# The output, up and down projections of a hybrid attention block: one planned list in place of an order written by hand

## The chip, the cores and the metric

The kernel runs on 1 core of one Trainium2 chip. Its engines run side by side, each through its own fixed queue of instructions: TensorE (PE in the profile, its weight loads PEld), VectorE (DVE), ScalarE (ACT) and GpSimd (POOL); SyncE (SP) issues the DMAs. An instruction that waits holds up all that is queued behind it on its engine. The metric is the device time in microseconds (us), the median of several runs.

## The reference

One layer on 2048 latent tokens of width 1024 and 256 context tokens, then a last RMS norm. The parts that the change touches come after attention and the delta rule:

```python
def conv_ffn(h, w_up, conv_w, conv_b, w_down):
    u = depthwise_conv(h @ w_up, conv_w) + conv_b
    gate, val = jnp.split(u, 2, axis=-1)
    return (jax.nn.silu(gate) * val) @ w_down
...
    lat_out = jnp.concatenate([o_attn, o_gdn], axis=-1) @ w_out
...
        x = x + g1 * lat_out
        x = x + g2 * conv_ffn(modulate(x, norm2_g[l], sh2, sc2), w_up[l], ffn_conv_w[l],
                              ffn_conv_b[l], w_down[l])
...
    return rms_norm(x, final_norm_g)
```

`o_attn` is normalised, `o_gdn` normalised and gated with SiLU(z). The up projection has 2 x 2816 columns, the convolution runs over three positions, and all values are float32.

## The kernel before

**Numbers.** Each float32 operand of these products is split into a float16 part and a float16 rest (`split`: ScalarE makes the first, GpSimd or VectorE the rest), and three matmuls (part by part, part by rest, rest by part) stand for one. Weights are scaled into the float16 range first, by a norm taken on the way: squares on ScalarE, sums on PE, a power of -0.5 on GpSimd, the scaling on ScalarE.

**Two ways to set an order.** The stages up to attention use `Plan` (lines 193 to 404). The program records operations through stand-ins for the engines (`add`) and tiles (`Lazy`); each gets its dependences, its tile's turn in a ring of buffers, and a modelled duration (`cost`, lines 226 to 258). `order` then walks through modelled time: each engine takes the recorded operation that can start first, and among equals the one recorded earlier ("work"). `issue` writes the instructions out in that order. The model's constants are `fixed` and `rate`: attention sets its own at line 1153, `(150, 55, 200, 170, 25)` and 2.34, and a `patience` for GpSimd and ScalarE; the class has `(65, 65, 0, 50, 42)`, 2.4 and none. By `cost`, VectorE takes `fixed[0] + n / 0.96` ns for n elements a partition and `fixed[1]` more for a scalar operand in memory; a two-input GpSimd operation with float16 result takes `60 + 1.95 n`. The three last stages (lines 1563 to 2345) don't use it. There the order of the calls is the order of the instructions, written by hand: generators are advanced one `yield` at a time between the matmuls, with `idle(n)` to put them back.

**Output projection** (`output`, line 1764). For the four token blocks of 512, in the order 1, 0, 2, 3, `mixed` loads the heads' outputs (line 1811), scales them on VectorE (lines 1831, 1834), transposes them on PE (line 1840) and splits them. `weights` makes the eight weight columns during the first block. Eight products of 24 matmuls (line 1934) give a block; VectorE adds the gated result to x (line 1945), and squares are summed for the second norm. `norm_tail` (line 1591) sums them on PE, takes the power on GpSimd (line 1581), spreads it over the partitions on PE (line 1587), scales the block and writes it to DRAM as `h2c`. `blocks` and `plain` read it back (line 1715) and make the up projection's right-hand operands.

**Up projection** (`up_stage`, line 2028). A block j of 2 x 128 columns is one 2 x 2 block product by a Strassen-like scheme with seven products P1 to P7 of 12 matmuls (line 2035) in place of eight; a step is one j with one half (sb) of the tokens. There are 22 x 2 steps. `parts_of` (line 1679) makes the seven left operands of a block: four sums on GpSimd (lines 1692 to 1702) and seven splits (ScalarE line 1614, GpSimd line 1615). A product accumulates onto one of three banks; what is read from a bank in between (line 2083 after P7, for one) must be read before the next product is added to it (P4, in the step after). PE's order in a step is P1, P6, P4 and P3 of the step before, P5, P2, P7. VectorE and ScalarE gather the results in two rows (`ue`), a single pair for all steps; `after` convolves them (ScalarE line 2103, VectorE line 2106 twice each), applies SiLU, splits the product and stores it as `hidc` (line 2122). `row` and `after` copy two border columns from step to step on GpSimd (lines 2052, 2109).

**Down projection** (lines 2267 to 2344). 96 units, each up to eight blocks of one output column for one token block; `leading` and `rest` scale and split the unit's weights two units ahead (four raw and four split buffers), `down` has the matmuls (line 2297). The last norm of a token block runs during the next. The last column is done in two halves, so that the first half's norm lies under the second half's products.

Of the kernel before, what the change touches and what calls it, by code (L numbers as in the profile page):

```python
# [20 lines left out]
P = 128  # L21
# [97 lines left out]
class Lazy:  # L119
# [30 lines left out]
    def bitcast(self, dtype):  # L150
        return self._next(self.shape, lambda x: x.bitcast(dtype), dtype=dtype)
# [270 lines left out]
def kernel(  # L422
# [1147 lines left out]
    p3a = ExitStack()  # L1570
    x3 = p3a.enter_context(tc.tile_pool(name="x3", bufs=2, side="right", reuse_waits="tile"))
    s3 = p3a.enter_context(tc.tile_pool(name="s3", bufs=2, side="right", reuse_waits="tile"))
    RAWB, WSB, XW = 4, 4, 514
    direct = Direct(nc)

    def rstd_made(e, rs_pool, ps, w, tag):

        n = w // P
        rc = e.tile(rs_pool, [P, 2 * n], F32, "nrc", f"nrc_{tag}", 2)
        e.V.tensor_scalar(out=rc, in0=ps[:, :2 * n], scalar1=1.0 / D, scalar2=EPS, op0=ALU.mult, op1=ALU.add)  # L1580
        e.G.tensor_tensor(out=rc, in0=rc, in1=mhalf.broadcast_to([P, 2 * n]), op=ALU.pow)  # L1581
        return rc

    def rstd_spread(e, ps_pool, ps_tag, ps_bufs, rc, w, tag):
        rs = e.tile(ps_pool, [P, 512], F32, ps_tag, f"nrs_{tag}", ps_bufs)
        for i in range(w // P):
            e.PE.matmul(out=rs[:, i * P:(i + 1) * P], lhsT=rc[:, 2 * i:2 * i + 1].broadcast_to([P, P]), rhs=ident, start=True,
                        stop=True)
        return rs[:, :w]

    def norm_tail(e, xv, tb, acc, pool, h2d, wait=1):

        ps = e.tile(psn, [P, 512], F32, "nps", f"nps_b{tb}", 1)
        for j in range(4):
            e.PE.matmul(out=ps[:, 2 * j:2 * j + 2], lhsT=acc[:, j * P:(j + 1) * P], rhs=ones[:, 0:2], start=True,
                        stop=True)
        dg = rstd_made(e, pool, ps, 512, f"b{tb}")
        for _ in range(wait):
            yield
        rs = rstd_spread(e, psn, "nps", 1, dg, 512, f"b{tb}")  # L1600
        yield
        for k in range(KT):
            e.V.scalar_tensor_tensor(out=xv[:, k, :], in0=xv[:, k, :], scalar=aff2[:, k:k + 1], in1=rs,
                                     op0=ALU.mult, op1=ALU.mult)
            e.S.activation(out=xv[:, k, :], in_=xv[:, k, :], func=AF.Identity, bias=mod2[:, 8 + k:9 + k])
            if k % 2:
                e.SY.dma_start(out=h2d[:, k - 1:k + 1, :], in_=xv[:, k - 1:k + 1, :])
            yield
# [3 lines left out]

    def split(lo_e, dst, src):
        S.copy(out=dst[0], in_=src)  # L1614
        lo_e.tensor_tensor(out=dst[1], in0=src, in1=dst[0], op=ALU.subtract)  # L1615
# [13 lines left out]
    up_w, raw_u = {}, {}  # L1629

    def fetch_up(j, rs=range(2)):
        if j < NJ:
            for r in rs:
                t = w3.tile([P, 2, 4, P], F32, tag="raw", name=f"raw_u{j}_{r}", bufs=RAWB)
                raw_u.setdefault(j, []).append(t)
                SY.dma_start(out=t.rearrange("p a k f -> p (a k) f"), in_=wu[2 * j + r])

    def scales(j, tag):

        g, v = raw_u[j]  # L1640
        ss = w3.tile([P, 2], F32, tag="uss", name=f"uss_{j}", bufs=2)
        sg = w3.tile([P, 8], F32, tag="usg", name=f"usg_{j}", bufs=2)
        fw = w3.tile([P, 8], F32, tag="ufw", name=f"ufw_{j}", bufs=3)
        junk = []
        for r, t in enumerate((g, v)):
            junk.append(s3.tile([P, 2, 4, P], BF16, tag=tag, name=f"junk_{j}_{r}", bufs=2))
            S.activation(out=junk[r], in_=t, func=AF.Square, accum_out=ss[:, r:r + 1])
            yield
        yield from idle(4)
        ps = pt3.tile([P, 512], F32, tag="pt", name=f"uns_{j}")  # L1650
        PE.matmul(out=ps[:, 0:2], lhsT=ones, rhs=ss, start=True, stop=True, skip_group_check=True)
        for r in range(2):
            for k in range(8):
                PE.matmul(out=ps[:, 2 + 2 * r:4 + 2 * r], lhsT=junk[r][:, k // 4, k % 4, :], rhs=ones16, start=k == 0, stop=k == 7,
                          skip_group_check=True)
        V.tensor_reduce(out=sg[:, 0:1], in_=ps[:, 0:2], axis=AX, op=ALU.add)
        V.tensor_scalar(out=sg[:, 0:1], in0=sg[:, 0:1], scalar1=WTOP ** -2, scalar2=1e-30, op0=ALU.mult, op1=ALU.add)
        V.tensor_scalar(out=sg[:, 1:3], in0=ps[:, 2:6].rearrange("p (r c) -> p r c", c=2)[:, :, 0], scalar1=1.0, scalar2=1e-30,  # L1658
                        op0=ALU.mult, op1=ALU.add)
        G.tensor_tensor(out=sg[:, 3:6], in0=sg[:, 0:3], in1=mhalf.broadcast_to([P, 3]), op=ALU.pow)  # L1660
        yield from idle(3)
        for t in (g, v):
            S.activation(out=t, in_=t, func=AF.Copy, scale=sg[:, 3:4])
            yield
        V.tensor_tensor(out=sg[:, 1:3], in0=sg[:, 1:3], in1=sg[:, 4:6], op=ALU.mult)
        V.tensor_tensor(out=sg[:, 1:3], in0=sg[:, 1:3], in1=reach[:, 2 * j:2 * j + 2], op=ALU.mult)
        V.tensor_tensor(out=sg[:, 1:3], in0=sg[:, 1:3], in1=offs[:, 2 * j:2 * j + 2], op=ALU.add)
        V.tensor_tensor(out=bet[:, j:j + 1], in0=sg[:, 1:2], in1=sg[:, 2:3], op=ALU.mult)
        V.reciprocal(out=sg[:, 6:7], in_=bet[:, j:j + 1])
        V.reciprocal(out=sg[:, 7:8], in_=sg[:, 3:4])  # L1670
        V.tensor_scalar(out=fw[:, 0:6], in0=cols[:, C_FC + 6 * j:C_FC + 6 * j + 6], scalar1=sg[:, 7:8], scalar2=hinv,
                        op0=ALU.mult, op1=ALU.mult)
        V.tensor_scalar(out=fw[:, 3:6], in0=fw[:, 3:6], scalar1=sg[:, 6:7], scalar2=DTOP, op0=ALU.mult, op1=ALU.mult)
        V.tensor_scalar(out=fw[:, 6:7], in0=cols[:, C_FB + 2 * j + 1:C_FB + 2 * j + 2], scalar1=sg[:, 6:7], scalar2=DTOP,
                        op0=ALU.mult, op1=ALU.mult)
        up_w[j] = fw
        yield

    def parts_of(j):

        g, v = raw_u.pop(j)
        w = [w3.tile([P, 4, 2, 4, P], F16, tag="ws", name=f"ws_u{j}_{i}", bufs=WSB) for i in range(2)]
        at = {n: w[i // 4][:, i % 4] for i, n in enumerate(TOP)}
        up_w[j] = at, up_w[j]
        a11, a12, a21, a22 = g[:, 0], g[:, 1], v[:, 0], v[:, 1]
        s = w[1][:, 3].rearrange("p f k t -> p (f k t)").bitcast(F32).rearrange("p (k t) -> p k t", k=4)

        def put(n, x):
            split(G, [at[n][:, f] for f in range(2)], x)

        put("A11", a11)
        G.tensor_tensor(out=s, in0=a21, in1=a22, op=ALU.add)
        yield
        put("S1", s)
        G.tensor_tensor(out=s, in0=s, in1=a11, op=ALU.subtract)
        G.tensor_tensor(out=a21, in0=a11, in1=a21, op=ALU.subtract)
        yield
        put("S2", s)
        yield
        put("A12", a12)  # L1700
        yield
        G.tensor_tensor(out=a12, in0=a12, in1=s, op=ALU.subtract)
        put("S3", a21)
        yield
        put("A22", a22)
        yield
        put("S4", a12)
        yield

    def staged(sb, n, tb, k0, raw=False):  # L1710
        if raw:
            t = w3.tile([P, 2, 512], F32, tag="raw", name=f"hst{sb}_{n}_{k0}", bufs=RAWB)
        else:
            t = s3.tile([P, 3, 512], F32, tag="oraw", name=f"hst{sb}_{n}_{k0}", bufs=3)[:, 0:2, :]
        SY.dma_start(out=t, in_=h2c[tb, :, k0:k0 + 2, :])
        return t

    def put(blk, n, kp, x, eng):
        split(eng, [blk[n][:, f, 2 * kp:2 * kp + 2] for f in range(2)], x)

    def plain(sb, blk, which):

        got = []
        for n, kp in which:
            tb, k0 = dict(B11=(0, 0), B21=(0, 4), B22=(1, 4))[n]
            got.append((n, kp, staged(sb, "p" + n, 2 * sb + tb, k0 + 2 * kp)))
            if len(got) == 2:
                yield
                put(blk, *got.pop(0), V)
# [677 lines left out]
```

## Time and profile before

| | us |
|---|---|
| median of 3 runs | 3478.06 (3476.42 to 3480.72) |
| the profiled execution, whole | 3474.39 |
| its span, first to last instruction | 3472.6 |
| output projection's body in it | 1781.2 to 2023.5 |
| up projection | 2023.5 to 2997.1 |
| down projection to the last pass | 2997.1 to 3459.2 |

The mean granted TensorE clock is 0.959 of full speed. In the profile a line like "PE ub L2035 <- DVE xa L2083: 71.0, 18, 4.3" says that TensorE stood still before instructions of line 2035 that write the tile ub, until VectorE had done line 2083, for 71.0 us in 18 times, the longest 4.3. In a timeline row stand start, duration, engine, line, operation, output and input, count, and in brackets the idle time before it and who ended it. Lines of planned stages are all 404, the line that issues them.

### The profile page before, as it was taken

How to read it: one execution, taken by the hardware profiler on the slowest of the kernel's cores; microseconds unless marked ns; L12 is line 12 of the kernel's file. 1: busy time of each engine (PE TensorE's matmuls, PEld its weight loads, DVE VectorE, ACT ScalarE, POOL GpSimd, SP SyncE). 2: the span in 40 equal slices, each digit the busy share in tenths (PEclk: the TensorE clock that was granted, in tenths of full speed). 3: DMA queues.
4: the chain of work that ended last, by engine and by line, in shares of the span. 5: the costliest groups of instructions: out<-in, count | busy, mean ns of one | idle time of the engine just before them, and what ended most of it. 6: DMA issues, size and time to landing. Idle time of an engine off the chain costs nothing.

```text
span 3472.6 us, 63367 instructions
## 1 busy us (share of the span) xinstructions
PE 3159.5 (91%) x25496; PEld 2010.1 (58%) x25496; DVE 2307.9 (66%) x3623; ACT 1731.2 (50%) x2665; POOL 1696.9 (49%) x1572
## 2 busy tenths in 40 slices
PE   6799999979999999999868788999988998999998
PEld 3799878857787777767634333444444443444444
DVE  5665677878777779889745656555555556656554
ACT  5443233457777777777643454454454444322221
POOL 4685455447767777777842344444444444000000
PEclk8999999989999999999989889999999999999999
DMA  6223335641222232322144432121221111654642
GB/s 233 88 67 97 121 112 146 195 127 56 82 92 72 88 99 87 103 82 78 50 151 164 161 139 86 61 69 60 71 69 61 61 62 40 244 185 147 209 142 87
DMA packets 241369, 377.00 MB, mean 109 GB/s; under 512 B 21561, under 2 KB 145049, under 8 KB 238241
## 3 DMA queue, kind: packets, MB, share of 16 engines
q1 hardware_dynamic: 239120, 367.52, 32.1%
q0 software_dynamic: 1952, 5.42, 0.6%
q8 instruction: 200, 3.28, 0.4%
q14 instruction: 97, 0.79, 0.1%
HBM read 262.13 MB, written 111.17 MB: 107 GB/s over the span
## 4 chain that ended last, share of the span: by engine, by line
PE 46%; DVE 17%; issue 12%; POOL 11%; ACT 7%; DMA 5%; SPq 0%; POOLq 0%; DVEq 0%; ACTq 0%
PE pdn L2297 13%; PE sc L404 6%; PE ops L404 5%; DVE cv L2106 5%; POOL ws_u L1615 3%; PE sm L404 3%; PE po L404 2%; PE ub L2035 1%; PE pa L404 1%; ACT cv L2103 1%; DVE mx L404 1%; DMA wm<-in_wm 1%; PE pg L534 1%; PE pg L535 1%; PE pg L533 1%
## 5 line engine op out<-in xcount | busy, mean ns | idle before, releaser
L404 POOL TENSOR_TENSOR lp<-p,hp 128x1024 f16<-128x1024 f32 x288 | 622.3, 2169 | 211.0 <-DVE hp L404 67.8
L2035 PEld LDWEIGHTS <-ws_u 128*128 128x128 f16 x3696 | 369.2, 100 | 556.0 <-issue 141.9
L404 DVE TENSOR_REDUCE mx<-sm 128x1 f32<-128x512 f32 x512 | 336.5, 682 | 64.1 <-PE sm L404 62.4
L404 ACT ACTIVATE p<-sc 128x1024 f32<-128x1024 f32 x288 | 295.3, 1025 | 135.5 <-PE sc L404 125.9
L2297 PEld LDWEIGHTS <-ws_d 128*128 128x128 f16 x2178 | 213.4, 98 | 250.5 <-ACT ws_d L1969 7.1
L2106 DVE SCALAR_TENSOR_TENSOR cv<-xa,ufw,cv 128x1024 f32<-128x1024 f32 (+1 forms) x172 | 242.0, 1417 | 166.9 <-ACT cv L2103 152.3
L2297 PE MATMUL pdn<-hid,ws_d 128*128 128x512 f16 (+1 forms) x1584 | 337.8, 373 | 0.0
L1969 ACT CAST ws_d<-raw_d 128x1024 f16<-128x1024 f32 (+1 forms) x96 | 93.5, 974 | 264.8 <-DVE raw_d L1967 220.5
L404 PE MATMUL sc<-q,kh 128*128 128x512 f16 x576 | 219.0, 380 | 5.1 <-ACT p L404 4.0
L404 PE MATMUL sc<-qx,kx 128*128 128x512 f16 x576 | 219.1, 380 | 0.0
L2035 PE MATMUL ub<-xb,ws_u 128*128 128x512 f16 x528 | 146.9, 437 | 67.3 <-DVE xa L2083 67.3
L404 ACT CAST hp<-p 128x1024 f16<-128x1024 f32 x192 | 201.1, 1048 | 3.5
L404 PE MATMUL ops<-vst,hp 128*128 128x65 f16 (+1 forms) x4608 | 191.6, 193 | 6.4 <-DVE vst L404 3.2
L404 PE MATMUL sm<-kh,q 128*128 128x512 f16 x512 | 175.2, 384 | 13.6 <-DVE mx L404 13.3
L404 PEld LDWEIGHTS <-hp 128*128 128x128 f16 x4608 | 169.9, 97 | 23.2 <-DVE hp L404 2.9
L2035 PE MATMUL ua<-blk_a,ws_u 128*128 128x512 f16 x792 | 181.7, 379 | 0.0
L1934 PE MATMUL po<-ol,ws_o 128*128 128x512 f16 x768 | 180.2, 392 | 0.0
L1615 POOL TENSOR_TENSOR ws_u<-raw_u,ws_u 128x512 f16<-128x512 f32 x110 | 153.1, 1407 | 43.7 <-ACT ws_u L1614 43.7
L1581 POOL TENSOR_TENSOR nrc_f<-nrc_f,mhalf 128x8 f32<-128x8 f32 x3 | 7.6, 2527 | 340.1 <-DVE nrc_f L1580 340.1
L1974 DVE TENSOR_TENSOR ws_d<-raw_d,ws_d 128x1024 f16<-128x1024 f32 (+1 forms) x96 | 108.8, 1134 | 78.1 <-ACT ws_d L1969 78.1
L1660 POOL TENSOR_TENSOR usg<-usg,mhalf 128x3 f32<-128x3 f32 x22 | 36.7, 1668 | 240.0 <-DVE usg L1658 240.0
L533 PE MATMUL pg<-hl,ws_g 128*128 128x512 f32 x384 | 152.9, 398 | 0.0
(695 smaller groups left out, 8000.3 us busy)
## 6 DMA issues: line engine op xcount, KB each, us to landing
raw_d<-in_wd SPq DMA_DIRECT2D x64, 512.0 KB
raw_u<-in_wu SPq DMA_DIRECT2D x44, 512.0 KB
hidc<-cv SPq DMA_DIRECT2D x86, 256.0 KB
tk<-gsc SPq DMA_DIRECT2D x34, 512.0 KB
tT<-gsc SPq DMA_DIRECT2D x66, 256.0 KB
wm<-in_wm SPq DMA_DIRECT2D x64, 256.0 KB
gsc<-kd SPq DMA_DIRECT2D x64, 256.0 KB
hid<-hidc SPq DMA_DIRECT2D x8, 2048.0 KB
```

Source lines behind the costliest of these rows:

```text
L404: fn(**{k: v.get() if isinstance(v, Lazy) else v for k, v in kw.items()})
L533: PE.matmul(out=ps, lhsT=hi_l(k), rhs=hi_r(k), start=st, stop=False)
L534: PE.matmul(out=ps, lhsT=hi_l(k), rhs=lo_r(k), start=False, stop=False)
L535: PE.matmul(out=ps, lhsT=lo_l(k), rhs=hi_r(k), start=False, stop=en)
L1615: lo_e.tensor_tensor(out=dst[1], in0=src, in1=dst[0], op=ALU.subtract)
L1660: G.tensor_tensor(out=sg[:, 3:6], in0=sg[:, 0:3], in1=mhalf.broadcast_to([P, 3]), op=ALU.pow)
L1934: PE.matmul(out=ps, lhsT=w[:, x, k, :], rhs=ols[tb][:, y, k, :], start=k + f == 0, stop=k == KT - 1 and f == 2)
L1969: S.copy(out=made[u][:, 0, :n], in_=raws[u][:, :n])
L1974: V.tensor_tensor(out=made[u][:, 1, :n], in0=raws[u][:, :n], in1=made[u][:, 0, :n], op=ALU.subtract)
L2035: PE.matmul(out=ps, lhsT=w[:, x, k, :], rhs=b[:, y, k, :], start=first and k + f == 0, stop=k == 3 and f == 2, skip_group_check=True)
L2106: V.scalar_tensor_tensor(out=f, in0=t[:, 1 - sb + i:1 - sb + i + W], scalar=s.fw[:, 3 * r + i:3 * r + i + 1], in1=f, op0=ALU.mult, op1=ALU ...
L2297: PE.matmul(out=pss[i][:, :c1 - c0], lhsT=ws[:, x, k, :], rhs=h[:, y, :], start=a + k + f == 0, stop=a + k == NJ - 1 and f == 2)
```

## The change

The three stages become one function, `flow(plan)`, that records all its operations in one plan. One call of `issue` sets the order, with "work" as its rule. One set of pools serves from the first to the last (before, two were closed after the up projection and two opened). `Flow` is `Plan` with a price for memsets, a price for DMAs at 300 GB/s in place of 360, and 30 ns for the small bfloat16 matmuls; `fixed`, `rate` and `patience` stay those of the class. The six matmuls of two k-steps, or the twelve of one product P, form a group that isn't broken up.

```diff
+        def parts_of(j):
...
             put("A11", a11)
-        G.tensor_tensor(out=s, in0=a21, in1=a22, op=ALU.add)
+            V.tensor_tensor(out=s, in0=a21, in1=a22, op=ALU.add)
...
-        G.tensor_tensor(out=s, in0=s, in1=a11, op=ALU.subtract)
-        G.tensor_tensor(out=a21, in0=a11, in1=a21, op=ALU.subtract)
+            V.tensor_tensor(out=s, in0=s, in1=a11, op=ALU.subtract)
+            V.tensor_tensor(out=a21, in0=a11, in1=a21, op=ALU.subtract)
...
-        G.tensor_tensor(out=a12, in0=a12, in1=s, op=ALU.subtract)
+            V.tensor_tensor(out=a12, in0=a12, in1=s, op=ALU.subtract)
...
         def row(s, r):
             t = ue[r]
-            if s.sb:
-                G.tensor_copy(out=t[:, 0:2], in_=carry[:, 2 * s.j + r, :])
-            else:
-                G.memset(t[:, 0:2], 0.0)
-            G.memset(t[:, 1026:1028], 0.0)
+            S.copy(out=t[:, 0:2], in_=carry[:, 2 * s.j + r, :] if s.sb else zero)
             return t
...
-                    G.tensor_copy(out=carry[:, 2 * j + r, :], in_=t[:, 1024:1026])
+                    S.copy(out=carry[:, 2 * j + r, :], in_=t[:, 1024:1026])
...
-                G.tensor_copy(out=tailc[:, j, :], in_=z[:, :, 0])
+                V.tensor_copy(out=tailc[:, j, :], in_=z[:, :, 0])
...
+        first, w0, w1 = mixes(order[0]), weights(0), weights(1)
+        for g, n in ((first, 8), (w0, 3), (first, 4), (w1, 3), (first, 4)):
+            for _ in range(n):
+                next(g)
+        plan.gate = len(plan.ops) - 1
...
-                tracks.append(blocks(0, blk0, 1, True))
-                tracks.append(chained(idle(4), scales(0, "osq"), idle(2), parts_of(0)))
-                tracks.append(chained(idle(16), scales(1, "osq")))
+                tracks.append(chained(*(plain(0, blk0, m, kp) for m, kp in (("B11", 0), ("B11", 1), ("B21", 0), ("B21", 1))),
+                                      blocks(0, blk0, 1, V, False), *(plain(0, blk0, "B22", kp) for kp in range(2))))
+                tracks.append(chained(scales(0), parts_of(0), scales(1), parts_of(1)))
...
-            pace = 2
+            pace = 1
             if n == 1:
-                drain(work)
-                fetch_up(2)
-                work = chained(idle(2), scales(2, "nacc"), wd_squares(0), wd_squares(1))
-            elif n == 3:
-                drain(work)
-                work = chained(idle(6), parts_of(2))
+                work = chained(scales(2), parts_of(2), wd_squares(0), wd_squares(1))
             elif n >= 4 and sb == 0 and j < NJ - 3:
                 drain(work)
-                if n == 4:
-                    fetch_up(3)
...
+                work = chained(scales(j + 1), parts_of(j + 1), *(wd_squares(q) for q in more))
...
-                finish(x2, tb, cuts[0], rs, range(0, 4))
+                finish(x2, tb, cuts[0], rs, range(0, KT))
                 down(1, *tails[2])
                 gated(1)
-                squares(1)
-                ps = sums(pt3, "pt", acc[:, 256:512], 256, "fin1")
-                finish(x2, tb, cuts[0], rs, range(4, KT))
...
+        plan.issue(dict(o=("work", 1.0)))
+
+    class Flow(Plan):
+
+        @staticmethod
+        def cost(eng, name, kw, rate, fixed):
+            if name == "memset":
+                return 100.0, 0.0
+            if name.startswith("dma_start"):
+                t = kw["out"]
+                return 60.0, int(np.prod(list(t.shape))) * (2 if t.dtype == F16 else 4) / 300.0
+            if eng == "PE" and name == "matmul" and kw["rhs"].dtype == BF16:
+                return 30.0, 0.0
+            return Plan.cost(eng, name, kw, rate, fixed)
+
+    flow(Flow(tc, psn, pt3, ps3))
```

Matmuls, splits and convolution stay as they were in number and shape. New work is six more reads of `h2c` (512 KB each): the first half's B11, B21 and B22 are staged by themselves (`plain`) in place of being made from tiles that `blocks` holds. Their rests are made on VectorE; before, GpSimd made four of the six. `bitcast` of a recorded tile now gives the shape that the new type has.

More of the change, by code (lines that the diff above doesn't have):

```diff
@@ L1591, in norm_tail @@
[L1591 to L1608, printed above, removed]
@@ L1627, in chained @@
             yield from x
[L1629 to L1647, printed above, removed]
-            yield
[L1649 to L1663, printed above, removed]
-            yield
[L1665 to L1677, printed above, removed]
@@ L1881, in output @@
-        w0, w1 = weights(0), weights(1)
-        first = together([mixed(1, i) for i in range(4)], 2)
-        for n, _ in enumerate(first):
-            if n == 1:
-                for _ in range(2):
-                    load_wo()
-            if n >= 2:
-                next(w0, None)
-            if n >= 4:
-                next(w1, None)
-        drain(w0)
-        drain(w1)
-        new_x(order[0])
-        blk0, blk1 = {}, {}
-        tracks, pend = [], None
+                yield from mixed(tb, i, ols[tb])
@@ L2028, in up_stage @@
-    def up_stage():
-        acc, xv, blk0, blk1, rest0, work = output()
-        def product(ps, w, b, first):
-            for k in range(4):
-                for f, (x, y) in enumerate(((0, 0), (0, 1), (1, 0))):
-                    PE.matmul(out=ps, lhsT=w[:, x, k, :], rhs=b[:, y, k, :], start=first and k + f == 0,
-                              stop=k == 3 and f == 2, skip_group_check=True)
+                blk0.update(four(mk(ol3, [P, 2, 2, 4, 512], F16, "ol", "blk0_a", 4), ("B11", "T2")))
@@ L2038, in up_stage @@
+            if not end:
+                drain(chained(*tracks))
+        rest = tracks
         class Step:
@@ L2271, with last_norm @@
+        def last_norm(x2, tb, acc):
+            yield
+            rc = sums(acc, 512, f"f{tb}")
+            yield
+            yield
+            rs = spread(rc, 512, f"f{tb}")
+            yield
+            finish(x2, tb, (0, 512), rs, range(0, 4))
+            yield
+            finish(x2, tb, (0, 512), rs, range(4, KT))
+            yield
+        pend, x2 = iter(()), None
         for u, (tb, b, a, n) in enumerate(units):
@@ L2300, in gated @@
-            def gated(i, b=b, x2=x2, pss=pss, cuts=cuts, xp=xp):
+                for k0 in range(0, n, 2):
+                    with plan.group():
+                        for k in (k0, k0 + 1):
+                            h = hids[tb][a + k]
+                            for f, (x, y) in enumerate(PAIRS):
+                                PE.matmul(out=pss[i][:, :c1 - c0], lhsT=ws[:, x, k, :], rhs=h[y][:, c0:c1],
+                                          start=a + k + f == 0, stop=a + k == NJ - 1 and f == 2, skip_group_check=True)
```

764 lines of the change are left out of this document (358 added, 406 removed).

## The prediction

> **What bounds the kernel now.** I read the page's engine row first, then the windows view, cut where the kind of TensorE work changes. Its columns: stretch, length, busy us (and instructions) of PE, PEld, DVE, ACT, POOL, granted clock, DMA share, GB/s.
>
> ```profile
> PE 3159.5 (91%) x25496; PEld 2010.1 (58%) x25496; DVE 2307.9 (66%) x3623; ACT 1731.2 (50%) x2665; POOL 1696.9 (49%) x1572
> ...
> 1781.20:2023.50 242.30, 198.77 (x962) 98.04 (x961) 141.45 (x203) 101.64 (x177) 80.60 (x76) 0.92 0.46 164
> 2023.50:2150.00 126.50, 96.56 (x419) 43.47 (x418) 76.80 (x91) 57.14 (x77) 54.84 (x54) 0.85 0.31 106
> 2150.00:2997.10 847.10, 769.28 (x3700) 347.21 (x3699) 495.32 (x683) 392.47 (x526) 362.77 (x449) 0.95 0.21 74
> 2997.10:3025.40 28.30, 21.66 (x90) 8.97 (x89) 15.43 (x14) 8.30 (x9) 0.19 (x1) 0.88 0.61 210
> 3025.40:3459.20 433.80, 433.59 (x2103) 206.52 (x2101) 248.47 (x273) 104.81 (x120) 8.59 (x4) 1.00 0.48 155
> ```
>
> The rows are: the body of the output projection, the first up steps, the other up steps, the hand-over to down, and down. In down PE is busy 433.59 of 433.80 us: nothing is to be had. In the others no engine is full, PE pauses, and the granted clock is under 1: the mark of an order that blocks, not of a full engine. PE's busy time hides part of it, because a matmul at a low clock is busy for longer. So I count the matmuls of the main lines (1934 in the body, 2035 in up) and price them at the full rate.
>
> ```profile
> 1781.20:2023.50 242.30, 179.94 (x768) 0.92 0.46 164
> ...
> 2023.50:2150.00 126.50, 92.90 (x384) 0.85 0.31 106
> 2150.00:2997.10 847.10, 752.25 (x3313) 0.95 0.21 74
> ...
> 2231.56 2.75 PE L2035 MATMUL uc<-blk_b,ws_u 128*128 128x512 f16 x12
> 2234.15 2.75 PE L2035 MATMUL ua<-blk_b,ws_u 128*128 128x512 f16 x12
> ```
>
> Twelve matmuls, one product, start 2234.15 - 2231.56 = 2.59 us after the last: 0.2158 us each. PE's other work in a stretch is its busy time less that of the main line. Lost time of each:
> - Body: 768 x 0.2158 = 165.7, other 198.77 - 179.94 = 18.8, together 184.5 of 242.3: **57.8 lost**.
> - First up steps: 384 x 0.2158 = 82.9, other 3.7, together 86.6 of 126.5: **39.9 lost**.
> - Other up steps: 3313 x 0.2158 = 714.9, other 17.0, together 731.9 of 847.1: **115.2 lost**.
> - Hand-over: 90 x 0.2158 = 19.4 of 28.3: **8.9 lost**.
>
> Together 221.8 us. The waits view says whom PE waited for (us in total, times, longest), and the timeline shows one case from end to end.
>
> ```profile
> PE ub L2035 <- DVE xa L2083: 71.0, 18, 4.3
> PE pto L1840 <- DVE oraw L1831: 18.9, 7, 5.8
> PE nrs_b L1587 <- POOL nrc_b L1581: 12.9, 1, 12.9
> PE ub L2035 <- ACT blk_b L1614: 12.4, 1, 12.4
> PE nps_b L1595 <- DVE nacc_b L509: 10.3, 1, 10.3
> ...
> 2223.35 5.25 PE L2035 MATMUL ub<-xb,ws_u 128*128 128x512 f16 x12 [3.94 <-DVE xa L2083]
> 2251.09 0.68 DVE L2092 TENSOR_TENSOR xa<-uc,u 128x512 f32<-128x512 f32 x1
> 2255.48 1.26 POOL L1702 TENSOR_TENSOR raw_u<-raw_u,ws_u 128x512 f32<-128x512 f32 x1
> 2256.78 0.62 ACT L1614 CAST ws_u<-raw_u 128x512 f16<-128x512 f32 x1 [2.43 <-POOL raw_u L1702]
> 2257.30 1.24 ACT L2103 ACTIVATE cv<-xa,cols,ufw 128x1024 f32<-128x1024 f32 x1
> 2258.58 6.18 DVE L2106 SCALAR_TENSOR_TENSOR cv<-xa,ufw,cv 128x1024 f32<-128x1024 f32 x4 [6.81 <-ACT cv L2103]
> 2266.00 0.69 DVE L2083 TENSOR_TENSOR xa<-ub,s 128x512 f32<-128x512 f32 x1
> 2266.74 4.04 PE L2035 MATMUL ub<-xb,ws_u 128*128 128x512 f16 x12 [3.94 <-DVE xa L2083]
> ```
>
> Read it upwards. PE stands 3.94 us because product P4 may not write its bank before VectorE has read it (line 2083). VectorE is late because four convolution steps came just before, after a wait of 6.81 us for ScalarE. ScalarE had the rows of the convolution at 2251.09 + 0.68 = 2251.77 and took them at 2257.30: its queue held a weight cast that waited for a GpSimd sum (line 1702). So weights for the next block, due much later, hold up this step. This comes once in 43.39 us (2223.35 to 2266.74), one pair of steps.
>
> **Part by part.**
>
> *Other up steps.* The change takes out this chain twice over. Four sums (lines 1692 to 1702) go from GpSimd to VectorE, and the planner puts each operation where its modelled inputs are ready. Is there room? In this stretch there are 20 blocks. VectorE gets the four sums and a two-column tail copy per block, priced at 0.69 each by the 512-wide row above (which reads PSUM; the sums read SBUF): 69 us, so 564; ScalarE gets six two-column copies per block, not in the trace; between 0.19 and 0.62 us each (the cheapest and the narrowest rows below and above) they make 23 to 74 us, so 415 to 467; GpSimd falls. Against 731.9 us of PE work that is 77% and 57 to 64%: PE is what binds, and the copies lie under it, at up to 0.62 us each where that cover fails.
>
> The copies also bring ScalarE a wait that GpSimd had, for the convolution to have read the row (last row of the next fence: 28.2 us in 32 times, 0.9 each). Behind it in ScalarE's queue stand the row's own eviction, which waits for the same reads, and the next block's casts; 40 x 0.9 = 36 us fit into its free 36%. SyncE's queue: with four raw buffers the next block's loads go out about a block (43 us) before use, against landings of 6 to 7 us (below), so a hidden store ahead of them costs nothing; zero.
>
> ```profile
> 2226.15 0.19 ACT L1647 ACTIVATION_READ_ACCUMULATOR junk<-raw_u 128x1 f32 x1
> ...
> 1400.00:1500.00 100.00, 94.05 (x1372) 70.45 (x1370) 86.37 (x145) 69.98 (x92) 76.13 (x40) 1.00 0.29 91
> 1500.00:1600.00 100.00, 96.32 (x1429) 72.02 (x1426) 84.33 (x144) 74.00 (x97) 74.29 (x39) 0.98 0.28 88
> 1600.00:1700.00 100.00, 97.77 (x1446) 74.42 (x1445) 85.19 (x137) 75.34 (x94) 78.99 (x40) 1.00 0.17 54
> ...
> L1615 POOL TENSOR_TENSOR ws_u<-raw_u,ws_u 128x512 f16<-128x512 f32 x82 | 110.2, 1361 | 1.5 <-ACT ws_u L1614 1.5
> L2106 DVE SCALAR_TENSOR_TENSOR cv<-xa,ufw,cv 128x1024 f32<-128x1024 f32 x64 | 98.0, 1551 | 110.3 <-ACT cv L2103 107.1
> ...
> POOL xa L2055 <- DVE cv L2106: 28.2, 32, 1.3
> ```
>
> How well does a planned list do? The attention stage, planned by the same code, keeps PE busy for 94.05, 96.32 and 97.77 of 100 us, with VectorE at 85%, fuller than here. But its model has constants of its own; the new list uses the class's defaults, and by these a GpSimd split costs 60 + 512 x 1.95 = 1058 ns, a convolution step 65 + 1024 / 0.96 + 65 = 1197. The trace has 1361 and 1551. A list made with short durations has operations in the queue before their inputs are there. So I take 95%, under the mean: 731.9 / 0.95 = 770.4, 38.5 lost, **76.7 gained**. Bounds: 97.77% (16.7 lost) and 94.05% (46.3).
>
> What do the pauses left over cost?
>
> ```profile
> 2068.31 0.59 PE L1651 MATMUL uns<-uss,k 128*128 128x2 f32 x2 [2.81 <-ACT junk L1647]
> 2069.19 5.28 PE L2035 MATMUL ua<-blk_b,ws_u 128*128 128x512 f16 x12
> 2074.26 3.04 PE L2035 MATMUL ub<-blk_T,ws_u 128*128 128x512 f16 x12
> ```
>
> A pause of 2.81 us made the next product last 2074.26 - 2069.19 = 5.07 us in place of 2.59: it cost 2.81 + 2.48 = 5.29. [...]
>
> *Body.* Its pauses are of order too: a transpose issued ahead of its VectorE scaling (18.9 us), the norm's spread behind GpSimd's power (12.9), both able to stand behind ready products. What stays is the start, where each weight column must be loaded, squared and scaled. I leave 25 lost: **32.8 gained**. Bounds: 96% busy (184.5 / 0.96, 8 lost) and 45 lost. The new list stages six more tiles of 512 KB; 3.1 MB at the body's 164 GB/s is 19 us of DMA, beside a DMA share of 0.46: hidden, and up to 19 if it is not, since these tiles feed the first up step.
>
> *First up steps.* The path is the last norm, its write to DRAM, the reads back, then the blocks for the second half. The reads:
>
> ```profile
> 1938.99 6.23 DMA hst_b<-h2c
> 2056.62 7.16 DMA hst_b<-h2c
> ```
>
> PE has two steps, 14 x 2.59 = 36 us, to fill that path, and in a planned list four more products that need no difference block (10 us). Today's path also holds pauses that the order makes (10.3, and part of 12.4). I leave 20 lost: **19.9 gained**; bounds 8 and all 39.9. [...]
>
> *Hand-over, down, tail.* Down's prices, buffers (four raw, four split) and order stay: zero, under VectorE's 248 of 433.8 us. Hand-over 8.9 to 6, **2.9 gained** (bounds 3 and 8.9). At the end, eight scalings of the first half now stand together ahead of the last gate:
>
> ```profile
> 3457.07 1.66 DVE L2237 SCALAR_TENSOR_TENSOR x<-x,cols,nrs_fin 128x256 f32<-128x256 f32 x4 [2.86 <-PE nrs_fin L1587]
> 3459.03 0.48 DVE L2302 SCALAR_TENSOR_TENSOR x<-pdn,mod,x1p 128x256 f32<-128x256 f32 x1 [0.31 <-PE pdn L2297]
> ```
>
> Eight take 3.3 us and end at 3460.4, so the gate comes **1.4 later** (bounds 0 and 1.7).
>
> *Sum:* 76.7 + 32.8 + 19.9 + 2.9 - 1.4 = 130.9 us. The profiled execution took 3474.39 us (span 3472.6), the median of the runs is 3478.06, 3.67 more. Profiled after: 3343.5; median: 3347.2. With the good bounds together (98.5 + 49.8 + 31.9 + 5.9 - 1.4 = 184.7) 3293; with the bad ones (68.9 + 12.8 + 0 + 0 - 1.7 = 80.0) 3398.
>
> **Rivals.**
> - *Half the up pauses stay.* The short durations make ScalarE or VectorE stand ahead of the convolution in about every second pair, and body and first steps gain nothing: 115.2 / 2 - 1.4 = 56 gained, 3422. For: 1361 against 1058. Against: VectorE 23% free. Chance 0.12.
> [...]
> - *No change.* The one pair of convolution rows stays single; if its release (convolution read, then the next eviction) were the real cycle, another wait would take the old one's place: 3478. Against: ScalarE's lag of 5.5 us explains the pause alone. Chance 0.03.
> - *Slower.* Sums and splits of weights stand ahead of line 2083 in VectorE's fixed queue in every step, not once per pair. A pause with its slow product costs 3.94 + 2.48 = 6.4 us; 40 of them are 257 lost in place of 115.2, 142 more, and with the other gains, 32.8 + 19.9 + 2.9 - 1.4 = 54.2: about 3566. It decides when the loss per pair exceeds (115.2 + 54.2) / 20 = 8.5 us. Against: VectorE has its one pause per pair now, and the list staggers such work. Chance 0.09.
>
> **Numbers.** The forecast has 0.66. Faster by over 0.2% (7 us, about what a measurement here can tell from none): 0.66 + 0.12 + 0.10 = 0.88; within 0.2%: 0.03; slower: 0.09. The range goes from 3296, the forecast's good end, to 3422, the first rival.
>
> **What would show it.** Right: waits of PE for line 2083's successor under 20 us, clock 0.98 or more in up, PE's pauses for transposes gone, the up steps 770 us long. Down stays at 434. Wrong: a PE wait of some 4 us in every step; VectorE over 85% in up; a long wait of PE for the second half's blocks; a DMA share over 0.7 in the body.

## The result, and the profile after

| | median us (lowest to highest) | ratio to before, 95% interval |
|---|---|---|
| before, on the same chip | 3479.39 (3476.42 to 3484.18) | |
| the planned list | 3281.97 (3278.77 to 3283.9) | 0.943 [0.9414, 0.9447] |

The forecast was 3347, in a range from 3296 to 3422. The time fell by 197, not by 131. The profiled execution took 3278.77 us, its span is 3276.8, and the mean granted clock rose from 0.959 to 0.979. The engine row and the windows of the planned kernel, cut at the same borders as before (ahead of the body stands the ramp, from attention's last matmul):

```profile
PE 3106.2 (95%) x25496; PEld 1995.0 (61%) x25496; DVE 2395.4 (73%) x3737; ACT 1747.1 (53%) x2797; POOL 1550.0 (47%) x1241
...
1745.90:1771.50 25.60, 10.22 (x46) 7.66 (x47) 17.07 (x31) 15.65 (x38) 18.32 (x22) 0.54 0.73 257
1771.50:1958.40 186.90, 185.96 (x959) 94.63 (x960) 144.54 (x217) 100.94 (x172) 78.44 (x73) 0.99 0.64 232
1958.40:2065.00 106.60, 91.81 (x438) 42.34 (x436) 79.90 (x104) 58.04 (x86) 29.67 (x19) 0.94 0.39 132
2065.00:2803.10 738.10, 732.72 (x3653) 337.09 (x3651) 576.04 (x769) 405.36 (x639) 242.75 (x152) 1.00 0.26 86
2803.10:2825.00 21.90, 21.90 (x103) 9.97 (x102) 19.73 (x21) 9.92 (x10) 0.00 (x0) 1.00 0.70 222
2825.00:3262.80 437.80, 437.58 (x2122) 208.30 (x2119) 246.50 (x266) 102.03 (x119) 6.55 (x4) 1.00 0.48 150
3262.80:3276.80 14.00, 1.80 (x8) 1.45 (x8) 5.28 (x14) 0.42 (x1) 1.01 (x1) 0.65 0.44 150
```

In the body and in the other up steps PE is now busy for over 99% of the stretch, at a clock of 0.99 and 1.00. Stage by stage:

| | before | after | change | forecast |
|---|---|---|---|---|
| up to attention's last matmul | 1753.4 | 1745.9 | -7.5 | 0 |
| ramp | 27.8 | 25.6 | -2.2 | 0 |
| output's body | 242.3 | 186.9 | -55.4 | -32.8 |
| first up steps | 126.5 | 106.6 | -19.9 | -19.9 |
| other up steps | 847.1 | 738.1 | -109.0 | -76.7 |
| hand-over | 28.3 | 21.9 | -6.4 | -2.9 |
| down | 433.8 | 437.8 | +4.0 | 0 |
| tail | 13.4 | 14.0 | +0.6 | +1.4 |

Most of the first row is the change too, though the operations of those stages are the same. From the delta rule's last matmul (1700.5 us before, 1698.8 after) to attention's last one, the kernel before takes 52.9 us and so does e1, the other order by hand below; the planned kernels take 46.1 to 49.4, this one 47.3. There the output projection's first loads and scalings stand among attention's last operations, and the list puts them in other places. So some 5.6 of the 7.5 us are a gain that the forecast had at 0; what an execution has won or lost up to 1700 us is spread.

In the row of the other up steps 6.5 us only moved: 43 matmuls of the down projection lay in that stretch before and 13 do now, 30 x 0.2158 us, and hand-over and down have them instead. The excess over the forecast stands in the body, 22.6 us, and in the other up steps, 32.3, or 25.8 without what moved.

Whom PE waits for from 1740 us to the end (total, times, longest):

```profile
PE pto L406 <- DVE oraw L406: 14.4, 7, 5.8
PE nps_b L406 <- DVE nacc_b L406: 5.1, 1, 5.1
PE uns L406 <- ACT junk L406: 4.1, 1, 4.1
PE ub L406 <- ACT blk_b L406: 3.8, 1, 3.8
PE ops L406 <- POOL lp L406: 3.0, 3, 1.2
PE ub L406 <- DVE xa L406: 2.8, 3, 1.5
```

All planned stages have the one line 406, so one goes by the tiles (ub, uc and ua are the up projection's banks). The wait that stood on top, PE for the read of P4's bank, is down from 71.0 us in 18 times to 2.8 in 3. Of the transposes' 14.4 us, 13.6 lie in the ramp; in the body there is one wait of 0.8. One step of the planned list, rows of VectorE and PE from its timeline:

```profile
2402.89 2.17 DVE L406 TENSOR_TENSOR cv<-cv,cv 128x1025 f32<-128x1025 f32 x1
...
2404.99 0.68 DVE L406 TENSOR_TENSOR xa<-ub,s 128x512 f32<-128x512 f32 x1
...
2405.59 1.04 DVE L406 TENSOR_TENSOR raw_u<-raw_u,raw_u 128x512 f32<-128x512 f32 x1
2405.72 2.75 PE L406 MATMUL ub<-blk_T,ws_u 128*128 128x512 f16 x12 [0.19 <-DVE xa L406]
```

The eviction after P7 (xa from ub) ends at 2405.67, and P4 starts at 2405.72: just in time, with nothing in hand. The weight sum (raw_u) stands behind the eviction. In the other step of the pair the eviction ends over 3 us early.

### The profile page after: what moved, and what is told of

The parts are those of the page before. It is cut to its first block, busy times and chain, and to the rows that moved or that the text cites. A ratio compares the mean times of both kernels' runs of the same rounds, so it can differ in the third digit from the quotient of the medians.

```text
span 3276.8 us, 63242 instructions
## 1 busy us (share of the span) xinstructions
PE 3106.2 (95%) x25496; PEld 1995.0 (61%) x25496; DVE 2395.4 (73%) x3737; ACT 1747.1 (53%) x2797; POOL 1550.0 (47%) x1241
## 3 DMA queue, kind: packets, MB, share of 16 engines
q1 hardware_dynamic: 239984, 370.67, 34.8%
## 4 chain that ended last, share of the span: by engine, by line
PE 72%; DVE 12%; POOL 5%; DMA 4%; ACT 3%; issue 3%; SPq 0%; POOLq 0%; DVEq 0%; ACTq 0%
PE pdn L406 14%; PE ub L406 9%; PE sc L406 6%; PE uc L406 6%; PE ua L406 6%; PE po L406 6%; PE ops L406 5%; PE sm L406 3%; PE pa L406 1%; DVE cv L406 1%; DVE mx L406 1%; PE pg L531 1%; PE pg L530 1%; PE pg L532 1%; ACT p L406 1%
## 5 line engine op out<-in xcount | busy, mean ns | idle before, releaser
L406 PEld LDWEIGHTS <-ws_u 128*128 128x128 f16 x3696 | 361.7, 99 | 444.2 <-issue 23.9
L406 DVE SCALAR_TENSOR_TENSOR cv<-xa,ufw,cv 128x1025 f32<-128x1025 f32 (+1 forms) x176 | 251.8, 1486 | 61.2 <-ACT cv L406 61.2
L406 POOL TENSOR_TENSOR ws_u<-raw_u,ws_u 128x512 f16<-128x512 f32 x110 | 181.2, 1655 | 197.4 <-ACT ws_u L406 156.0
L406 PE MATMUL po<-ol,ws_o 128*128 128x512 f16 x768 | 173.4, 382 | 0.0
L406 POOL TENSOR_TENSOR usg<-usg,mhalf 128x3 f32<-128x3 f32 x22 | 20.0, 909 | 285.4 <-DVE usg L406 285.4
L530 PE MATMUL pg<-hl,ws_g 128*128 128x512 f32 x384 | 152.8, 398 | 0.0
L532 PE MATMUL pg<-hl,ws_g 128*128 128x512 f32 x384 | 152.3, 397 | 0.0
```

Source lines behind the costliest of these rows:

```text
L406: fn(**{k: v.get() if isinstance(v, Lazy) else v for k, v in kw.items()})
L530: PE.matmul(out=ps, lhsT=hi_l(k), rhs=hi_r(k), start=st, stop=False)
L532: PE.matmul(out=ps, lhsT=lo_l(k), rhs=hi_r(k), start=False, stop=en)
```

## The experiments

The theory after the result: PE stood still through the order alone, and the planned list gains because it puts weight work behind the eviction that frees PE's bank. Its rivals: the gain comes from the sums' move to VectorE alone; from PE's matmuls being rearranged; or from free room on engines. Four runs took the change apart, six changed the model's durations, and the rest asked how much room VectorE has, and what an order costs. Stage lengths below are taken as in the table above, from the main line's first and last matmuls; the first up steps are its first 384. The last column counts waits for the evictions (tiles xa and u).

| run | median us | body | first up | other up | PE ub <- DVE: us, times |
|---|---|---|---|---|---|
| before | 3478.06 | 242.3 | 126.5 | 847.1 | 71.0, 18 |
| planned list | 3281.97 | 186.9 | 106.6 | 738.1 | 2.8, 3 |
| e1, hand order, sums on VectorE | 3408.96 | 242.4 | 123.3 | 780.9 | 34.8, 20 |
| e2, list, sums on GpSimd | 3305.13 | 187.1 | 109.6 | 753.7 | 11.8, 19 |
| e10, list, PE in recorded order | 3300.26 | 197.2 | 107.7 | 740.1 | 4.2, 3 |
| e7, list by "path" | 3491.95 | 212.6 | 118.4 | 863.4 | 87.7, 36 |
| e4, attention's durations | 3275.17 | 185.2 | 105.4 | 733.6 | 5.1, 3 |
| e8, e4 and dearer two-input work | 3280.72 | 185.5 | 108.5 | 739.1 | 5.5, 2 |
| e6, durations x 1.5 | 3300.64 | 186.4 | 106.9 | 771.2 | 14.1, 4 |
| e13, x 0.9 | 3291.33 | 191.1 | 105.7 | 740.0 | 3.8, 3 |
| e12, x 0.75 | 3398.66 | 199.0 | 112.3 | 833.6 | 70.5, 22 |
| e5, x 0.5 | 3446.69 | 209.0 | 110.9 | 871.1 | 117.5, 22 |
| e11_1, 2 more additions a step, planned | 3282.0 | 186.8 | 105.1 | 737.0 | 4.7, 4 |
| e11_2, 4 more, planned | 3300.85 | 187.2 | 109.0 | 755.9 | 5.4, 5 |
| e14, 4 more, not planned | 3382.34 | 187.0 | 106.3 | 833.8 | 77.1, 25 |
| e9, e4 and patience | 3274.28 | 185.6 | 101.8 | 733.7 | 3.0, 2 |
| e15, planned list again | 3282.95 | 186.6 | 105.4 | 738.6 | 2.8, 3 |
| e16, e9 again | 3272.97 | 185.7 | 101.8 | 733.7 | 3.0, 2 |

**The sums by hand (e1).** Kernel before, with one part of the change: four lines of `parts_of`.

```diff
-        G.tensor_tensor(out=s, in0=a21, in1=a22, op=ALU.add)
+        V.tensor_tensor(out=s, in0=a21, in1=a22, op=ALU.add)
```

and so for the other three sums.

> The order written by hand, with one edit: the four sums of the weights' parts go from GpSimd to VectorE. Theory Q (the GpSimd sums are the cause: ScalarE's casts wait for them and the convolution waits behind the casts): the pause of some 4 us per pair of steps goes, PE's wait for line 2083 falls from 71 us to under 20, and the time to about 3380. Theory O (the order of the queues is the cause, whichever engine has the sums): the casts stay ahead of the convolution in ScalarE's queue and now wait for VectorE; at least half of the 71 us stays, 3425 to 3480.

Measured: 3408.96 us, ratio 0.9795 [0.9778, 0.9812]. The other up steps became 66 us shorter, the body not at all. PE's waits in this kernel, the second row from its body alone (18.9 before):

```profile
PE ub L2035 <- DVE xa L2083: 34.8, 20, 6.6
PE pto L1840 <- DVE oraw L1831: 18.1, 6, 5.8
```

The result lies between what the two theories gave. The same pause still comes once a pair, at 1.25 us for 3.94, and in one case followed through (at 2251.72 us) ScalarE takes the convolution's rows 0.1 us after they are there, where it came 5.5 us late. So ScalarE's wait for the GpSimd sum was the greater part of the up steps' loss, as the prediction's chain of rows said, and that part can be had without a list.

**The list without the sums' move (e2), and PE not rearranged (e10).** e2 is the planned kernel with those four lines back on `G`. In e10 the other engines are planned as in the change, but PE takes only the oldest operation that it has left:

```diff
+                if e == "PE" and self.fifo:
+                    cand = [i for i in cand if i == self.fifo[-1]]
```

> The planned list, with the four sums back on GpSimd. Theory Q: the pauses come back in part, some 2 us a pair, 3310 to 3340. Theory O: the list puts the casts where the sums are done, PE waits no more than in the planned kernel, 3282 within 6.

> The planned list, but PE must take its operations in the order in which they are recorded; the other engines are planned freely. If PE's look-ahead is what removes the pauses (theory L): 3300 to 3350, pauses in every pair. If the order of the other queues is (O): the up steps after the first stay within 5 us of the planned kernel's 738, and only the body and the first up steps lose, some 10 to 25 us together: about 3295.

Measured: 3305.13 (0.9495 [0.9478, 0.9512]) and 3300.26 (0.9484 [0.9465, 0.9503]). e2 again lies between its theories, e10 near its second. With the sums left on GpSimd the list still takes 93 us out of the other up steps; with both it is 109 (6.5 of each only moved). Either part alone breaks most of the chain, so their gains (66 and 93) don't add up to 109. The order alone isn't all, then: which engine makes the sums is worth 66 us by hand and 16 in the list. Rearranging PE is worth 10 us of the body's 55 and 2 us of the other up steps (5, since 12 more of down's matmuls lie in the planned kernel's). In e10 the 308 up products even stand in exactly the order that they had by hand, and the other up steps take 740.1 us in place of 847.1: what gains there is the order of the other engines. For the body e10 shows less. Its recorded order of PE isn't the hand-written one, since the transposes stand elsewhere between the products, so how the other 45 us are shared between that order and the other engines' queues stays open.

**The rule (e7).** One word: the ready operation with the longest modelled path behind it goes first, in place of the one recorded first.

```diff
-        plan.issue(dict(o=("work", 1.0)))
+        plan.issue(dict(o=("path", 1.0)))
```

> The planned list with the rule path (what has the longest chain behind it goes first) in place of work (what is recorded earlier). What is left to win in the planned kernel is some 20 us in the first up steps, which hang on a chain, and 10 elsewhere. If the rule matters: first up steps under 100, total 3265 to 3278. If PE's time is all that counts: 3282 within 5; it may be slower by up to 20 if products of later steps are held back.

Measured: 3491.95 us, ratio 1.0034 [1.0021, 1.0047], a little slower than the order by hand and far outside all that was expected. PE waits in it:

```profile
PE ub L406 <- DVE u L406: 69.7, 27, 4.0
PE pto L406 <- DVE oraw L406: 24.8, 3, 13.7
PE ub L406 <- DVE xa L406: 18.0, 9, 5.7
```

So a planned list as such gains nothing: this one has the same operations, pools and sums on VectorE and the same copies on ScalarE, and is 210 us longer than the change.

**The durations (e4, e8, e6, e5, e12, e13).** The prediction feared that short modelled durations leave 38.5 us of pauses. These kernels have the same operations, and in their model other constants. e4 and e8 start from

```diff
-    flow(Flow(tc, psn, pt3, ps3))
+    listed = Flow(tc, psn, pt3, ps3)
+    listed.fixed = (150, 55, 200, 170, 25)
+    flow(listed)
```

and e8 also makes two-input work dearer, by 1.4 on GpSimd and 1.15 on VectorE. In the planned kernel's other up steps a convolution step on VectorE took 1491 ns on average, 1.17 of e4's 1272: 1283 where GpSimd was busy for under a tenth of it (100 steps), 2144 where for over nine tenths (19). The others have, with 0.5 (e5), 0.75 (e12), 0.9 (e13) or 1.5 (e6),

```diff
-            return Plan.cost(eng, name, kw, rate, fixed)
+            d, move = Plan.cost(eng, name, kw, rate, fixed)
+            return (d if eng in ("PE", "SY") else 0.5 * d), move
```

> The planned list, made with the fixed costs that attention's list uses (150, 55, 200, 170, 25), nearer to the durations in the trace. If short modelled durations cost something (theory S, the 5% of the prediction): faster than the planned kernel by 5 us or more, under 3277. If a list bound by PE has slack for them (theory P): 3282 within 4.

> The planned list, made with attention's fixed costs, and GpSimd's two-input operations at 1.4 and VectorE's at 1.15 of their modelled time, as the trace shows them when both run at once. If what is left of the pauses in the up steps comes from durations that are short (theory S, small): up steps 730 to 733, total 3270. Theory P: no further gain over the list with attention's constants, 3275 within 4.

> The planned list, made with the same durations raised by half, so that by the model VectorE is over-full in the up steps. Theory S: the list is late everywhere, the planner lets PE's products slip back; up steps 760 or more, total over 3310. Theory P: the order stays workable, total 3280 to 3300.

> The planned list, made with VectorE's, ScalarE's and GpSimd's durations halved. Theory S (short durations cost what the prediction gave them): a list that is short by half, not by a tenth, loses far more: up steps 780 to 850 us, total over 3330. Theory P (a stage with slack on the other engines takes almost any list): up steps within 15 us of 738, total under 3305.

> The planned list, made with VectorE's, ScalarE's and GpSimd's durations at three quarters: short by a quarter more than in the planned kernel. With the halved list at 871 us in the up steps and the planned one at 738, a loss that grows evenly with the error (theory S) gives about 800, total about 3350; a loss that starts only where the slack of the other engines is used up (theory P) gives under 755, total under 3305.

> The planned list with the model's VectorE, ScalarE and GpSimd durations times 0.9. With the class's durations the other up steps took 738 us, with three quarters of them 834. Even-loss theory (each per cent by which the durations are too short costs PE something): 738 + 0.4 x 96 = 776 us, the whole about 3320. Step theory (nothing is lost until the list has put weight work ahead of the eviction that frees P4's bank): either 745 or less and the whole under 3290, or at once over 800 and the whole over 3345; nothing between.

Measured, as ratios: e4 0.9409 [0.9392, 0.9426], e8 0.9424 [0.941, 0.9438], e6 0.9481 [0.9466, 0.9497], e5 0.9899 [0.9884, 0.9914], e12 0.9763 [0.9747, 0.978], e13 0.9441 [0.942, 0.9461]. Better durations (e4) are worth some 4 us in the up steps and 7 in the whole. Dearer ones on top (e8) give nothing more: its 739.1 us hold 43 of down's matmuls where the change has 13, and 30 x 0.2158 = 6.5. Ten per cent shorter costs 2 us there and 4 in the body (e13's whole is 1.3 us over the bound set for the step, its up steps are within theirs). A quarter shorter costs 96 and a half 133, both more than either theory had; with the half, the up steps are longer than by hand. So the loss isn't even: 2 us for the first tenth, 94 more between 0.9 and 0.75. What happens there, in the timeline of e12:

```profile
2431.50 2.75 PE L406 MATMUL ub<-blk_b,ws_u 128*128 128x512 f16 x12
2432.73 1.64 DVE L406 TENSOR_TENSOR ws_u<-ws_u,raw_u 128x512 f32<-128x512 f32 x1
2434.29 1.22 DVE L406 TENSOR_TENSOR cv<-cv,cv 128x1025 f32<-128x1025 f32 x1
2435.43 1.64 DVE L406 TENSOR_TENSOR raw_u<-raw_u,ws_u 128x512 f32<-128x512 f32 x1
2436.99 0.68 DVE L406 TENSOR_TENSOR xa<-ub,s 128x512 f32<-128x512 f32 x1
```

Two weight sums of 1.64 us, due later, have passed ahead of the eviction, and P4 starts at 2437.72, after a pause of 3.47 us. That is the mechanism of the prediction's rival "slower", sums ahead of line 2083's successor, though it comes once per pair (22 waits) and not in every step. In e5, where the convolution's last step and the tail copy stand ahead of the eviction as well, this wait reaches 117.5 us, again in 22 times:

```profile
PE ub L406 <- DVE xa L406: 117.5, 22, 9.5
```

Too long durations aren't free either: in e6 the up steps take 771.2 us, with 73 of down's matmuls among them, 60 x 0.2158 = 13 us, so some 20 us go. One wait of 11.3 us for VectorE is in it; which order caused the rest I didn't trace.

**Room or place (e11, e14).** Additions whose results nobody uses are added to VectorE's work: two (e11_1) or four (e11_2) of 511 columns per step, recorded in the plan. The lines of e11_2, which stand in a loop over the two rows of the step (e11_1 has `range(1)`):

```diff
+                if (j, sb) != (0, 0):
+                    for _ in range(2):
+                        V.tensor_tensor(out=c[:, 1025:1536], in0=f[:, 0:511], in1=f[:, 511:1022], op=ALU.add)
```

e14 has the same four per step from block 2 on, but issued right ahead of the eviction after P7, unknown to the plan (the part that issues them):

```diff
+                        if i in self.late:
+                            x = args["out"]
+                            for _ in range(4):
+                                nc.vector.tensor_tensor(out=x[:, 0:511], in0=args["in1"][:, 0:511], in1=args["in1"][:, 1:512], op=ALU.add)
```

> The planned kernel with two more 511-wide additions on VectorE in each up step, results not used; the planner knows of them. VectorE's share of the up steps after the first goes from 78% to about 85%. Theory V (what a planned list loses is set by how full the fullest of the other engines is, and the prediction read its loss from attention's stretches at 85%): up steps 745 to 760. Theory P, taken strictly (PE's time alone counts as long as no engine is full): 738 within 4.

> The same with four more additions per step; VectorE to about 92%. Theory V: PE at 90 to 95%, up steps 770 to 810, total 3315 to 3355. Theory P, taken strictly: still under 750, total under 3295.

> The planned list, and in the steps of blocks 2 to 21 four additions of 511 columns on VectorE (some 0.65 us each, their result is not used) issued right ahead of the eviction after P7, without the plan knowing of them. e11_more_vector_2 has the same four per step, but planned. Amount theory (only VectorE's load counts): other up steps 756 us and the whole 3301, as there. Place theory (in one step of each pair the eviction comes just in time, so what stands ahead of it delays P4): 20 pauses of 2.6 us, other up steps about 790 (780 to 840 if the late evictions also cost clock), the whole 3330 to 3385, and a PE wait for that eviction of 40 us or more in some 20 times.

Measured: 3282.0 (0.9423 [0.9409, 0.9437]), 3300.85 (0.948 [0.9466, 0.9494]) and 3382.34 (0.9701 [0.9679, 0.9724]). The windows from 2100 to 2750 us of e11_1, e11_2 and e14, in this order:

```profile
2100.00:2750.00 650.00, 645.59 (x3243) 298.15 (x3242) 541.38 (x756) 367.38 (x579) 218.48 (x144) 1.00 0.24 74
```

```profile
2100.00:2750.00 650.00, 633.24 (x3178) 290.08 (x3177) 564.35 (x818) 360.62 (x572) 221.49 (x139) 1.00 0.23 71
```

```profile
2100.00:2750.00 650.00, 590.50 (x2894) 268.32 (x2893) 540.58 (x733) 329.84 (x520) 199.81 (x125) 0.97 0.21 65
```

At 541 / 650 = 83% VectorE cost PE nothing (e11_1); at 87% the other up steps were 18 us longer (e11_2), between what the two theories gave. e14 has the additions of e11_2, with VectorE at 83% of its longer steps, and loses 96. So the amount alone doesn't decide; the place does. Its wait and one case of it, VectorE's timeline:

```profile
PE ub L2236 <- DVE xa L2236: 77.1, 25, 4.1
```

```profile
2328.78 2.18 DVE L2236 TENSOR_TENSOR cv<-cv,cv 128x1025 f32<-128x1025 f32 x1
2330.88 3.83 DVE L2235 TENSOR_TENSOR xa<-s 128x511 f32<-128x511 f32 x4
2334.80 0.69 DVE L2236 TENSOR_TENSOR xa<-ub,s 128x512 f32<-128x512 f32 x1
```

The additions took 3.83 us, not the 2.6 expected, and PE's pause is 3.85: once per pair, where the eviction had nothing in hand.

**A better version (e9, e16), beside the change (e15).** e4 with attention's `patience` for GpSimd and ScalarE:

```diff
+    listed.fixed = (150, 55, 200, 170, 25)
+    listed.patience = PATIENCE
```

> The planned list with attention's fixed costs and its patience as well: GpSimd may wait 150 ns and ScalarE 100 for an operation that is more urgent. Both theories: 3275 within 4; faster by 5 or more would say that the greedy choice costs something here.

> The planned list as it was changed, once more, beside e16. 3282 within 4 us.

> The planned list with attention's durations and patience, as in e9_patience. If its gain of 8 us there is real: 3274 within 3 us and an interval wholly under that of e15; if it was chance: the intervals overlap.

Measured: e9 3274.28 (0.9406 [0.9391, 0.942]); on one chip e15 3282.95 (3282.07 to 3283.47, 0.9416 [0.9396, 0.9437]) and e16 3272.97 (3271.18 to 3274.8, 0.9387 [0.9366, 0.9407]). The two ratios' intervals overlap, from 0.9396 to 0.9407, so by the sign set beforehand it isn't decided; both carry the spread of the kernel before. The runs themselves lie 7 us apart. By them e16 is faster by about 0.3%, of which the first up steps give 3.6 us and the other up steps 4.9. What the patience adds to e4 isn't shown: in the whole, e9 and e4 overlap (3272.57 to 3275.03 and 3271.05 to 3277.58). e16 has the lowest median found.

## Why the prediction was right in sign and too small

- **"The mark of an order that blocks, not of a full engine."** Right. In the other up steps the prediction's 731.9 us of PE work are 725.4 without the 6.5 that moved, so PE loses 738.1 - 725.4 = 12.7 us in place of 115.2 (its row shows 5.4 idle), and in the body 186.9 - 184.5 = 2.4 in place of 57.8.
- **The chain** P4, line 2083, convolution, ScalarE's cast, line 1702: right, by e1, for the greater part. The weight work was in the wrong place; e12 and e14 bring the pauses back by putting work ahead of the eviction.
- **Room.** VectorE was forecast at 77% of the PE work: 576.04 / 738.1 = 78%, though two of the four sums take 1.06 and 1.64 us and not 0.69. ScalarE: 405.36 / 738.1 = 55%, just under the 57 to 64; a two-column copy costs 0.18 to 0.19 us, the low bound.
- **"So I take 95%, under the mean: 38.5 lost." This step failed.** Measured: 12.7 lost, PE at 98.3% in place of 95, and under the good bound of 16.7. It had two reasons, and both were off. The first was the three windows of attention at 94 to 98%. They were taken as "fuller than here", but that is what they lost by: from 1400 to 1500 us PE stood idle for 5.95, and 5.2 of that were waits for VectorE. The kernel before has four windows at this load of VectorE as well, from 900 to 1300; the best and the worst:

```profile
900.00:1000.00 100.00, 99.76 (x1457) 78.35 (x1456) 73.77 (x141) 79.00 (x108) 71.48 (x40) 1.00 0.25 82
...
1200.00:1300.00 100.00, 98.07 (x1448) 75.38 (x1444) 78.62 (x138) 78.93 (x106) 77.22 (x42) 1.00 0.27 89
```

At 74 to 79% for VectorE, PE is busy for 98 to 99.8: these rows give 2 to 14 lost. The second reason was the short durations. They are short indeed, and for the splits more so than the rows of before said, yet a list has only to keep the eviction ahead of the weight work, and it does so until they are some 10 to 25% shorter still; better ones (e4) gain only some 4 us there. The groups of the planned kernel's up steps:

```profile
L406 POOL TENSOR_TENSOR ws_u<-raw_u,ws_u 128x512 f16<-128x512 f32 x95 | 159.3, 1685 | 164.2 <-ACT ws_u L406 122.8 <-issue 41.4
L406 DVE SCALAR_TENSOR_TENSOR cv<-xa,ufw,cv 128x1025 f32<-128x1025 f32 x80 | 131.4, 1700 | 32.1 <-ACT cv L406 32.1
L406 DVE SCALAR_TENSOR_TENSOR cv<-xa,ufw,cv 128x1024 f32<-128x1024 f32 x80 | 98.1, 1282 | 27.4 <-ACT cv L406 27.4
```

A GpSimd split takes 1685 ns where the model has 1058, and PE doesn't feel it: GpSimd is busy for 242.75 us of 738.1.
- **Body, "I leave 25 lost".** Off the same way: 2.4. PE's waits in it fell from 18.9 us for transposes and 12.9 for the power to one of 0.8. The start with its weight columns, for which the 25 was left, costs the body nothing. 45 of the 55 gained come with PE's recorded order (e10). The six more tiles are hidden, at a DMA share of 0.64, under the 0.7 named.
- **First up steps:** 19.9, as forecast; the path over DRAM is still there, at a clock of 0.94. The 20 left was chosen between bounds of 8 and 39.9, so that it is met to a tenth is luck.
- **Up to attention's end:** put at 0 without a reason; some 5.6 us are the list's.
- **The range:** its lower end, 3296, is called the forecast's good end, but the good bounds add up to 3293. The measured 3281.97 lies under both, since body and up steps each beat their good bound: 2.4 lost against 8, and 12.7 against 16.7.
- **Hand-over and down:** together -2.4 against -2.9; without the 6.5 us of moved work -8.9, the whole loss of the hand-over. **Tail:** +0.6 against +1.4, and the eight scalings do stand ahead of the last gate, as said:

```profile
3260.65 3.22 DVE L406 SCALAR_TENSOR_TENSOR x<-x,cols,nrs_fin 128x256 f32<-128x256 f32 x8 [2.86 <-PE nrs_fin L406]
3263.79 0.48 DVE L406 SCALAR_TENSOR_TENSOR x<-pdn,mod,x1p 128x256 f32<-128x256 f32 x1
```

- **The rivals.** "Half the up pauses stay" didn't come; at three quarters of the durations (e12) a pause is back in about every pair. "Slower": its mechanism is real, as e12 and e5 show, but once per pair; with the class's durations it isn't reached. The 0.10 in the sum of the chances stood for pauses that cost no clock: no run shows that of pauses in general. In e1 the seventeen from 1.24 to 2.05 us cost none and one of 2.93 us did, as the last section tells; in the planned kernel nearly no pause was left for it to act on.

## What to carry to other kernels

Take an analogue at the same load of the other engines, or its loss is not yours. In the up steps the list gained by keeping one thing right, the background work behind the instruction that frees the scarce engine's next bank: find that instruction and how much it has in hand, for here the loss did not grow evenly with the errors of the model. Before planning everything, see whether one wait between two side engines holds the chain: here four changed lines gave 71 of the 197 us.

## What the runs showed of the hardware

Equal pauses of PE didn't cost the same here. Two rows of e14:

```profile
2294.65 2.75 PE L2236 MATMUL ub<-blk_T,ws_u 128*128 128x512 f16 x12 [3.86 <-DVE xa L2236]
...
2376.45 4.00 PE L2236 MATMUL ub<-blk_T,ws_u 128*128 128x512 f16 x9 [3.86 <-DVE xa L2236]
```

After a pause of 3.86 us the first product runs at the full rate, and the second has nine matmuls in 4.00 us, half the rate. Of the fifteen pauses of 3.85 or 3.86 us in e14's up steps, seven cost no clock, and the others made the next product 1.3 to 2.5 us longer. In e1 all seventeen pauses from 1.24 to 2.05 us ahead of an up product were free, and one of 2.93 us slowed the next product to 4.44.

The clock records of the traces show what parts them. In e14's up steps every stretch at half the clock lasts 3.41 or 6.83 us, and all begin on one grid of 3.41 us, as all 37 do in the records of before and all 16 in those of after. The windows of e14 cut on that grid, around the free pause and the slow one (behind the comma PE's busy time, further on the granted clock):

```profile
2289.29:2292.70 3.41, 1.50 (x7) 0.58 (x6) 3.34 (x4) 1.53 (x2) 1.78 (x1) 1.00 0.00 0
2292.70:2296.12 3.42, 1.47 (x7) 0.68 (x7) 3.28 (x6) 0.62 (x1) 0.20 (x1) 1.00 0.00 0
...
2371.21:2374.62 3.41, 1.38 (x7) 0.52 (x6) 3.34 (x4) 1.53 (x2) 1.66 (x1) 1.00 0.00 0
2374.62:2381.45 6.83, 5.00 (x12) 1.72 (x12) 6.69 (x10) 1.24 (x2) 2.45 (x2) 0.50 0.24 75
```

The free pause lies across two steps of the grid, with 1.91 and 1.95 us idle; the slow one leaves 3.41 - 1.38 = 2.03 us idle in one step, and the clock is halved behind it. Worked out in this way from PE's rows, all fifteen part so: the slow ones have 2.03 us or more idle in one step, the free ones 2.01 or less, and e1's pause of 2.93 has 2.74. In the up steps of the eighteen traces no step with over 2.01 us idle at full clock was followed by another at full clock, and all but two of the slow stretches (in e2 and e7) followed a step with 2.02 or more; in before, the full-clock steps that led to full clock had 2.00 us idle at most, the 19 that led to half had 2.02 at least. So in these traces the price of a pause went by how it lay on the grid, and the prediction's 2.48 us was one draw.

And the same addition of 512 columns on VectorE, one of the four weight sums (ws_u from raw_u), took between 0.68 and 1.64 us in the planned kernel (22 times, median 0.68). What it met there wasn't tried.
